# Activations side by side in a SwiGLU channel mixer, a token-major branch merge, and new durations in a list schedule

## The chip, the cores and the metric

The kernel runs on one core of a Trainium2 chip. The metric is the device time of one execution in microseconds (us), as the median of several runs. The profile is one execution taken by the hardware profiler. The engines are PE (TensorE, matrix products), ACT (ScalarE), DVE (VectorE), POOL (GpSimd) and SP (which issues the DMAs); PEld is TensorE's loading of the stationary operand.

## What is computed

One decoder block in float32 for 256 tokens and a model dimension of 1024: three token mixers side by side (sparse attention NSA with 16 heads, an mLSTM, cross-attention to 256 memory tokens), a gated merge, an output projection, and a SwiGLU channel mixer with 2816 hidden features.

```python
h = rmsnorm(x, g_pre_mix)
z = h @ w_in                        # 1024 -> 8248: queries, keys, values, gates of all mixers
...
y_nsa, y_ml, y_mem = ...            # (256, 1024), (256, 512), (256, 512)
gm = sigmoid(g_merge.reshape(B, S, 3, D_MODEL))
y = (gm[:, :, 0] * (y_nsa @ w_proj_nsa) + gm[:, :, 1] * (y_ml @ w_proj_ml)
     + gm[:, :, 2] * (y_mem @ w_proj_mem))
x = x + rmsnorm(y @ w_out, g_post_mix)
h = rmsnorm(x, g_pre_ffn)
gu = h @ w_ffn_in                   # 1024 -> 2 x 2816
gate, up = gu[..., :D_FF], gu[..., D_FF:]
x = x + rmsnorm((silu(gate) * up) @ w_ffn_down, g_post_ffn)
```

## The kernel before

**Numbers in two parts.** Every float32 operand of a large product is split into a high and a low part of the type float32r (`split`: ACT copies the high part, DVE subtracts to get the low one). A product is three matmuls: high by high, high by low, low by high (`mm3`).

**Weights.** They come as 162 units of [128, 1024] in the order of use, one DMA of 512 KB each (`fetch`, tile `raw`, four buffers), and each unit is split into `whi` and `wlo` (four buffers each).

**Two ways to form a product.** With features on the partitions (`fmaj`, `fpair`), a 128x128 block of weights is the stationary operand and the activations of all 256 tokens stream through: 24 matmuls of 256 columns for a tile of 128 features over the 8 tiles of the model dimension. With tokens on the partitions (`tmaj`), a 128x128 block of activations is stationary and 512 columns of weights stream through. `tmaj` works on both halves of the tokens (`tb`), so it holds two PSUM banks at a time and takes each unit of weights first for the one half, then for the other.

**PSUM.** There are eight banks: two with the tag `d`, three `s`, two `t` (transposes), one `v`. `ps_ds` gives out the five of `d` and `s` in turn.

**Stages, in program order.** Memory keys and values; compressed keys and values; gates; memory attention; attention keys and values; then the attention by four groups and two halves of the tokens (`nsa_half`), after each of which `fill` takes some tasks of the list `ORDER`, as many as `FILL` says: mLSTM tasks, then the letters `m`, the merge gates. Before, an `m` is `merge_pair`: two feature tiles of a gate in one bank (12 of them). The merge then goes by eight feature tiles: products of the three branches with their projections, times the sigmoids of the gates, summed and split into `yh` and `yl`. Then come the output projection `w_out` by tokens, the residual `x1` and its transposes, `xh` and `xl`, and the channel mixer: the first 512 gate and up features by tokens (`ffn_gate`, `ffn_up`), the other 18 feature tiles of either kind in pairs by features (`ffn_in`), and the down projection by tokens.

**The order of issue.** The instructions are first recorded in program order. `Plan.schedule` then simulates the engines with a duration for each instruction (`Plan.cost`) and latencies between engines (`LAT`, `SAME`), and on every engine takes the ready instruction that comes first in the program. Buffers of a tag are given out in program order. A tag is made once, with the number of buffers that its first tile names. `issue` then emits all instructions in the order found; no engine can change it at run time.

Of the kernel before, what the change touches and what calls it, by code (L numbers as in the profile page):

```python
# [10 lines left out]
F32 = mybir.dt.float32  # L11
# [6 lines left out]
P = 128  # L18
S = 256          # tokens
D = 1024  # L20
KD = D // P      # feature tiles of the model dimension
# [6 lines left out]
FILL = (5, 7, 1, 2, 3, 1, 3, 2)  # L28
ORDER = "qqvqqsghhhhfmmmmmmmmmmmm"
# [3 lines left out]
# columns of w_in  # L33
C_Q, C_KV, C_G, C_ML, C_IF, C_O, C_QM, C_MG = 0, 1024, 2560, 2608, 4144, 4152, 4664, 5176

# columns of the array of constants
K_ID, K_TRI, K_RV, K_BM, K_M0, K_C1, K_MT, K_END = 0, 128, 256, 257, 261, 533, 549, 677
# columns of the array of gains and small weights
# [4 lines left out]
class View:  # L43
    """A part of a tile that has no place yet."""
# [53 lines left out]

    def region(self):
        """First and last partition, and the elements of a partition as bits."""  # L100
        t = self.tile
        key = repr(self.steps)
        if key not in t.regions:
            p = int(self.ix.flat[0]) // t.n
            bits = np.zeros(t.n, bool)
            bits[self.ix[0].ravel() % t.n] = True
            t.regions[key] = (p, p + self.shape[0], int.from_bytes(np.packbits(bits).tobytes(), "big"))
        return t.regions[key]


class Slot:
    """A tile of the plan: its place is chosen when its first instruction is issued."""
# [50 lines left out]
class Plan:  # L163
    """Records the instructions in program order, with what they read and write, and issues them
    in the order of a list schedule: on every engine the ready one that comes first in the
    program. Tiles of a tag get their buffers in program order."""
# [8 lines left out]
    @contextmanager  # L175
    def later(self, n):
        """The instructions inside come as if n places later in the program."""
        self.boost -= n
        yield
        self.boost += n  # L180
# [47 lines left out]
    def cost(op):  # L228
# [14 lines left out]
        pointers = sum(v.n == 1 for v in op.ins)  # L243
        if op.eng == "ACT":
            return (50 if psum else 95) + 0.833 * n + 93 * ("accum_out" in op.kw or pointers > 0)
        if op.eng == "DVE":
            fast = not psum and op.method in ("tensor_copy", "tensor_scalar")
            return 67 + (0.52 if fast else 1.04) * n + 60 * pointers
# [6 lines left out]
        return 100 + 1.4 * n if op.method == "tensor_scalar" else 150 + 2.1 * n  # L255
# [9 lines left out]
    def schedule(self):  # L265
# [10 lines left out]
        def offer(op):  # L276
            """Makes op a candidate if its new tiles can have places; else it waits for the tag."""
            r = op.ready
            for t in op.tiles:
                if t.real is None:  # L280
                    tag = t.tag
                    if tag.next != t.seq or not tag.free:
                        tag.waiting.setdefault(t.seq, []).append(op)
                        return
                    r = max(r, tag.free[0][0])
            avail[op.eng].append((max(r, held(op)), op))

        def held(op):
            """A bank of PSUM serves one engine at a time, and so do the ports that GpSimd shares."""
# [96 lines left out]
def block_kernel(ctx, tc, order, xN, xT, memT, cst, vec, row, wg, w1, w2, W, out):  # L386
# [75 lines left out]
    def fmaj(out, xs, ks, wu, b0=0, first=True, last=True):  # L462
        """out [128 features, 256] += blocks of a unit (from b0) times the tiles ks of xs."""
# [5 lines left out]

    def fpair(xs, w, i, ps_new=ps_d):  # L470
        """[128, 2, 256]: the i-th pair of feature tiles of the weights w."""
        ps = ps_new([P, 2, S])
        for j in range(2):
            fmaj(ps[:, j, :], xs, range(KD), unit((w, 2 * i + j)))
        return ps

    def tmaj(xs, *key, n=4, ps_new=ps_d, into=None, last=0):
        """[128 tokens, 512] for both halves of the tokens, from n units of two feature tiles each; the
        last ones are used for the first half of the tokens before the second."""
# [29 lines left out]
    def warm_up(n):  # L509
        """Products of no use, that bring the tensor engine's clock up while it would wait."""  # L510
# [4 lines left out]
    def colsum(sq):  # L515
        """[128, 2]: per token, the sum of sq [128, 2, 256] over the partitions and the tiles."""
# [7 lines left out]
    def bcast(r, ps):  # L524
        """ps [128, 256]: the column r [128, 2] of the tokens, on every row."""
# [114 lines left out]
    msk = one.tile([P, 416], BF16, name="msk")          # m0 (272), c1 (16), mt (128)  # L640
# [56 lines left out]
    # running sums of logf, and i - sums  # L697
# [34 lines left out]
    # columns: selected keys 128-255, 0-127, compressed keys, window keys 0-127, 128-255  # L732
    kh = bigt("KK", 2, [P, NG, 528], F32R, "kh")
    kl = bigt("KK", 2, [P, NG, 528], F32R, "kl")
# [61 lines left out]
    for h2 in range(2):  # L796
        pvm = ps_v([P, 2, S], "pvm")
        ptm = [[work.tile([P, 2, S], F32R, tag=f"pT{i}", bufs=2, name="pTm") for i in range(2)] for _ in range(2)]
        for tb in range(2):
# [18 lines left out]
            pt = ps_t([P, 2, 2, P], "ptx")          # m tile, head, t  # L818
# [102 lines left out]
    gm = [bigt("G", 3, [P, 8, S], F32, f"gm{b}") for b in range(3)]  # L921

    def merge_pair(i):
        ps = fpair(X, "g_merge", i)
        ACT.activation(gm[i // 4][:, 2 * (i % 4):2 * (i % 4) + 2, :], ps, AF.Copy)
# [20 lines left out]
    def nsa_half(g, tb, qs, yT):  # L946
# [71 lines left out]
        for e in range(2):  # L1018
# [5 lines left out]
             "h": ml_head, "f": lambda _: ml_finish(), "m": merge_pair}  # L1024
# [16 lines left out]
    last_exp = exps[-12:]  # L1041

    def sigmoids(i):
        for b in range(3):
            g2 = gm[b][:, 2 * i:2 * i + 2, :]
            ACT.activation(g2, g2, AF.Sigmoid, after=last_exp)
# [3 lines left out]
    for fi in range(8):  # L1050
        ps = ps_s([P, 2, S], "pnl")
        pn_, pl_, pm_ = ps[:, 0, :], ps[:, 1, :], ps_t([P, S], "pmm")
        if fi % 2 == 0:
            sigmoids(fi // 2)
        w = unit(("proj", 2 * fi + 1))
        fmaj(pl_, yml, range(4), w)
        fmaj(pm_, ymem, range(4), w, 4)
        fmaj(pn_, (ynh, ynl), range(8), unit(("proj", 2 * fi)))
        m = work.tile([P, 3, S], F32, tag="p", bufs=2, name="mrg")
        for b, x in enumerate((pn_, pl_, pm_)):  # L1060
            DVE.tensor_mul(m[:, b, :], x, gm[b][:, fi, :])
        for b in (1, 2):
            DVE.tensor_add(m[:, 0, :], m[:, 0, :], m[:, b, :])
        split(yh[:, fi, :], yl[:, fi, :], m[:, 0, :])

# [9 lines left out]
    def scaled(name, xs, n, g, z, scale, pre):  # L1075
        """z [128 tokens, 2, 1024]: the products with the units of a name times the gains g and, per token,
        pre; yields per half of the tokens 1/rms of the products times the root of scale."""
# [17 lines left out]
    xh = bigt("KK", 2, [P, KD, S], F32R, "xh")  # L1095
    xl = bigt("KK", 2, [P, KD, S], F32R, "xl")
# [34 lines left out]
    for tb in range(2):  # L1131
# [7 lines left out]
        split(us[0][:, 0, :, t], us[0][:, 1, :, t], pt)  # L1139
    for i in range(4, KF):  # L1140
        ps = fpair((xh, xl), "ffn_in", i, ps_ds)
        sl_ = work.tile([P, S], F32, tag="sq", bufs=3, name="silu")
        DVE.tensor_mul(sl_, ps[:, 0, :], rfb)
        ACT.activation(sl_, sl_, AF.Silu)
        DVE.tensor_mul(sl_, ps[:, 1, :], sl_)
        u = us[i // 4]
        split(u[:, 0, i % 4, :], u[:, 1, i % 4, :], sl_)
# [19 lines left out]
def _layout(inputs):  # L1167
# [10 lines left out]
    def blocks(w, cols, k0=0, k1=None):  # L1178
        """[128, k, cols] of the rows k0..k1 (tiles)."""
# [23 lines left out]
    add_f("g_merge", w_in, tiles(C_MG, 24))  # L1203
    pn, pl, pm = a["w_proj_nsa"][0], a["w_proj_ml"][0], a["w_proj_mem"][0]
    for i in range(8):
        c = slice(i * P, (i + 1) * P)
        units["proj", 2 * i] = blocks(pn, c).reshape(P, 1024)
        units["proj", 2 * i + 1] = np.concatenate([blocks(pl, c), blocks(pm, c)], axis=1).reshape(P, 1024)
    for h in range(2):
        add_t("w_out", a["w_out"][0][:, 512 * h:512 * h + 512], h)  # L1210
# [38 lines left out]
def _stream(units, order):  # L1249
    """The units in the order of their use."""  # L1250
# [27 lines left out]
```

## Time and profile before

| | |
|---|---|
| median of 3 runs | 562.84 us (562.7 to 563.62) |
| profiled execution, span from first to last instruction | 561.4 us |
| mean granted TensorE clock | 0.996 |
| busy: PE, PEld, DVE, ACT, POOL | 551.9, 516.5, 404.5, 334.2, 36.0 us |
| matmuls | 3964 |

The times are of executions without the profiler; of the profiled execution the span is known, which leaves out what lies before its first and after its last instruction. Busy time of PE is the union of matmuls that overlap each other: the profiler gives a matmul of 256 columns some 284 ns from start to end, though the next one starts earlier. All large instructions are recorded by one helper line (L382), so groups are told apart by the names of their tiles: `pd`, `pss`, `pnl` and `pmm` are PSUM banks of large products, `pt...` those of transposes.

### The profile page before, as it was taken

The page shows a single profiled execution, that of the slowest core. Times are in us where ns is not written, and L with a number is a line of the kernel's source. Part 1 is how long each engine was busy: PE and PEld are TensorE (multiplying, and loading weights), DVE is VectorE, ACT ScalarE, POOL GpSimd, SP SyncE. Part 2 cuts the span into 40 slices and gives each one's busy share as a digit, 9 for nine tenths or more (in the row PEclk, how much of TensorE's full clock was granted, in tenths as well). Part 3 has the DMA queues.
Part 4 walks back from the last instruction along what each step waited for, and adds up shares of the span by engine and source line. Part 5 has one row for each costly group of instructions (what it writes and reads, how often), then busy time and mean ns, then how long its engine had stood idle before and what let it go on. Part 6 is the DMA issues. An engine that isn't in the chain of part 4 may idle for free.

```text
span 561.4 us, 10304 instructions
## 1 busy us (share of the span) xinstructions
PE 551.9 (98%) x3964; PEld 516.5 (92%) x3964; DVE 404.5 (72%) x802; ACT 334.2 (60%) x658; POOL 36.0 (6%) x44
## 2 busy tenths in 40 slices
PE   8999999999999999999999999999999999999994
PEld 8899998998989999999999998878999999988883
DVE  4897398598897989987786877865565656654543
ACT  6775677566596858777697444774444444444430
POOL 1110000002002011302111000000000000000000
PEclk9999999999999999999999999999999999999998
DMA  7994327617345253434435655744555545556522
GB/s 246 356 350 154 113 86 228 205 56 238 129 121 180 76 178 124 135 119 160 151 117 158 216 189 188 257 156 123 177 189 183 182 175 179 186 185 191 189 71 75
DMA packets 29281, 95.28 MB, mean 170 GB/s; under 512 B 3376, under 2 KB 6704, under 8 KB 28976
## 3 DMA queue, kind: packets, MB, share of 16 engines
q1 hardware_dynamic: 29232, 94.63, 51.5%
q8 instruction: 31, 0.51, 0.4%
q14 instruction: 18, 0.15, 0.1%
HBM read 92.52 MB, written 1.05 MB: 167 GB/s over the span
## 4 chain that ended last, share of the span: by engine, by line
PE 92%; DMA 3%; ACT 2%; DVE 2%; issue 0%; SPq 0%; DVEq 0%; ACTq 0%
PE pd L382 46%; PE pss L382 23%; PE pnl L382 6%; PE sc L382 3%; PE pvn L382 3%; PE pmm L382 2%; PE ptn L382 2%; DMA memt<-in_memT 2%; PE ph L382 2%; ACT whi L382 1%; DMA raw<-in_W 1%; PE pw L382 1%; PE pn L382 1%; PE pgf L382 1%; PE psm L382 1%; PE pvm L382 1%
## 5 line engine op out<-in xcount | busy, mean ns | idle before, releaser
L382 DVE TENSOR_TENSOR wlo<-raw,whi 128x1024 fp32r<-128x1024 f32 (+1 forms) x161 | 195.4, 1217 | 102.1 <-ACT whi L382 100.7
L382 ACT ACTIVATE whi<-raw 128x1024 fp32r<-128x1024 f32 (+1 forms) x161 | 167.6, 1046 | 164.3 <-issue 72.3
L382 PE MATMUL pd<-hh,whi 128*128 128x256 f32 x416 | 119.7, 288 | 0.3 <-DVE vs L382 0.3
L382 PE MATMUL pd<-hh,wlo 128*128 128x256 f32 x416 | 119.7, 288 | 0.0
L382 PE MATMUL pd<-hl,whi 128*128 128x256 f32 x416 | 119.5, 287 | 0.0
L382 PEld LDWEIGHTS pd<-hh,whi 128*128 128x128 f32 x416 | 79.5, 191 | 0.8 <-DVE vs L382 0.7
L382 PEld LDWEIGHTS pd<-hl,whi 128*128 128x128 f32 x416 | 79.4, 191 | 0.1
L382 PEld LDWEIGHTS pd<-hh,wlo 128*128 128x128 f32 x416 | 79.4, 191 | 0.0
L382 PE MATMUL pss<-xh,wlo 128*128 128x256 f32 x160 | 45.4, 284 | 0.0
L382 PE MATMUL pss<-xl,whi 128*128 128x256 f32 x160 | 45.4, 284 | 0.0
L382 PE MATMUL pss<-xh,whi 128*128 128x256 f32 x160 | 45.4, 283 | 0.0
L382 PE MATMUL pss<-whi,u 128*128 128x512 f32 x132 | 42.4, 392 | 0.0
L382 PE MATMUL pd<-xh,whi 128*128 128x256 f32 x128 | 36.2, 283 | 0.0
L382 PE MATMUL pd<-xl,whi 128*128 128x256 f32 x128 | 36.2, 283 | 0.0
L382 PE MATMUL pd<-xh,wlo 128*128 128x256 f32 x128 | 36.2, 283 | 0.0
L382 PEld LDWEIGHTS pss<-xh,whi 128*128 128x128 f32 x160 | 30.7, 192 | 0.0
L382 PEld LDWEIGHTS pss<-xl,whi 128*128 128x128 f32 x160 | 30.7, 192 | 0.0
L382 PEld LDWEIGHTS pss<-xh,wlo 128*128 128x128 f32 x160 | 30.7, 192 | 0.0
L382 PEld LDWEIGHTS pss<-whi,u 128*128 128x128 f32 x132 | 24.8, 188 | 5.5
L382 ACT ACTIVATE pp<-sc,mx 128x128 f32<-128x128 f32 (+1 forms) x64 | 27.1, 439 | 0.4 <-DVE mx L382 0.3
L382 PE MATMUL pss<-wlo,u 128*128 128x512 f32 x66 | 25.9, 392 | 0.0
L382 DVE TENSOR_REDUCE mx<-sc 128x1 f32<-128x16 f32 (+2 forms) x96 | 22.6, 284 | 3.3 <-PE sc L382 3.0
(306 smaller groups left out, 1243.9 us busy)
## 6 DMA issues: line engine op xcount, KB each, us to landing
raw<-in_W SPq DMA_DIRECT2D x159, 512.0 KB, 3.4
w<-in_w SPq DMA_DIRECT2D x2, 1024.0 KB, 7.0
raw<-in_W SPq DMA_DIRECT2D x6, 256.0 KB, 5.6
xt<-in_xT SPq DMA_DIRECT2D x2, 512.0 KB, 7.6
x<-in_xN SPq DMA_DIRECT2D x2, 512.0 KB, 4.9
out<-z SPq DMA_DIRECT2D x8, 128.0 KB, 2.0
memt<-in_memT SPq DMA_DIRECT2D x6, 128.0 KB, 5.4
wgt<-in_wg SPq DMA_DIRECT2D x1, 512.0 KB, 6.3
```

Of the source, the lines that this page charges most:

```text
L382: op.ins_ = getattr(op.real, op.method)(*map(arg, op.a), **{k: arg(x) for k, x in op.kw.items()})
```

## The change

**Channel mixer.** `xh` and `xl` become the two halves of one tile `xc` [128, 8, 2, 256] (and the attention's `kh` and `kl`, which hold its place before, two halves of `kk_`). For the 36 feature tiles of `ffn_in`, a new `fcat` multiplies each block of high weights with `xc[:, k]`, 512 columns at once, and the low weights with the high activations alone, 256 columns. The bank then holds two partial sums; `joined` copies the second with ACT and adds the first with DVE. Each feature tile has a bank of its own, where a gate and an up tile shared one.

**Merge by tokens.** The merge gates and the three projections are formed with `tmaj`, in halves of 512 features. `merge_half` replaces `merge_pair` (six instead of twelve), the merged result is by tokens and is transposed back, sixteen 128x128 transposes into banks `pty`, before the split. `ORDER` has 6 letters `m`, and `FILL` places one after each of the last six attention halves. The weights are laid out to match; their number of units stays 162.

**Durations.** `Plan.cost` gets other figures for ACT, DVE and POOL, and a new term for instructions on a part of the partitions.

```diff
-FILL = (5, 7, 1, 2, 3, 1, 3, 2)
-ORDER = "qqvqqsghhhhfmmmmmmmmmmmm"
+FILL = (5, 7, 1, 1, 1, 1, 1, 1)
+ORDER = "qqvqqsghhhhfmmmmmm"
...
+    def place(self):
+        return int(self.ix.flat[0]) // self.tile.n % P, self.shape[0]
...
+        part = any(v.place() != (0, P) and v.shape[0] >= 32 for v in op.outs + [v for v in op.ins if v.n > 1])
         if op.eng == "ACT":
-            return (50 if psum else 95) + 0.833 * n + 93 * ("accum_out" in op.kw or pointers > 0)
+            return ((50 if psum else 95) + 10 + 0.833 * n + 93 * ("accum_out" in op.kw) + 93 * (pointers > 0)
+                    + 110 * part)
         if op.eng == "DVE":
             fast = not psum and op.method in ("tensor_copy", "tensor_scalar")
-            return 67 + (0.52 if fast else 1.04) * n + 60 * pointers
+            return 71 + (0.52 if fast else 1.04) * n + 60 * (0 if n == 1 else pointers) + 100 * part
...
-        return 100 + 1.4 * n if op.method == "tensor_scalar" else 150 + 2.1 * n
+        return 100 + 1.4 * n if op.method == "tensor_scalar" else 2.1 * n - 70
...
+    def fcat(xc, w, ps):
+        hi, lo = unit(w)
+        b = lambda k: slice(k * P, (k + 1) * P)
+        for k in range(KD - 1):
+            PE.matmul(ps, hi[:, b(k)], xc[:, k], start=k == 0, stop=False)
+        for k in range(KD):
+            PE.matmul(ps[:, 0, :], lo[:, b(k)], xc[:, k, 0], start=False, stop=False)
+        PE.matmul(ps, hi[:, b(KD - 1)], xc[:, KD - 1], start=False, stop=True)
+        return ps
...
-    kh = bigt("KK", 2, [P, NG, 528], F32R, "kh")
-    kl = bigt("KK", 2, [P, NG, 528], F32R, "kl")
+    kk_ = bigt("KK", 1, [P, 2, NG, 528], F32R, "kk")
+    kh, kl = kk_[:, 0], kk_[:, 1]
...
-    gm = [bigt("G", 3, [P, 8, S], F32, f"gm{b}") for b in range(3)]
-    def merge_pair(i):
-        ps = fpair(X, "g_merge", i)
-        ACT.activation(gm[i // 4][:, 2 * (i % 4):2 * (i % 4) + 2, :], ps, AF.Copy)
+    gm = [bigt("G", 3, [P, 2, D], F32, f"gm{b}") for b in range(3)]
+    def merge_half(i):
+        b, h = i % 3, i // 3
+        for tb, ps in enumerate(tmaj(X, "g_merge", b, h)):
+            ACT.activation(gm[b][:, tb, 512 * h:512 * h + 512], ps, AF.Copy)
...
-    def sigmoids(i):
-        for b in range(3):
-            g2 = gm[b][:, 2 * i:2 * i + 2, :]
-            ACT.activation(g2, g2, AF.Sigmoid, after=last_exp)
-    for fi in range(8):
-        ps = ps_s([P, 2, S], "pnl")
-        pn_, pl_, pm_ = ps[:, 0, :], ps[:, 1, :], ps_t([P, S], "pmm")
-        if fi % 2 == 0:
-            sigmoids(fi // 2)
-        w = unit(("proj", 2 * fi + 1))
-        fmaj(pl_, yml, range(4), w)
-        fmaj(pm_, ymem, range(4), w, 4)
-        fmaj(pn_, (ynh, ynl), range(8), unit(("proj", 2 * fi)))
-        m = work.tile([P, 3, S], F32, tag="p", bufs=2, name="mrg")
-        for b, x in enumerate((pn_, pl_, pm_)):
-            DVE.tensor_mul(m[:, b, :], x, gm[b][:, fi, :])
-        for b in (1, 2):
-            DVE.tensor_add(m[:, 0, :], m[:, 0, :], m[:, b, :])
-        split(yh[:, fi, :], yl[:, fi, :], m[:, 0, :])
+    for h in range(2):
+        c = slice(512 * h, 512 * h + 512)
+        m = [work.tile([P, 1024], F32, tag="p", bufs=2, name="mrg") for _ in range(2)]
+        for b, name, xs, n in ((1, "proj_ml", yml, 2), (2, "proj_mem", ymem, 2), (0, "proj_nsa", (ynh, ynl), 4)):
+            g2 = gm[b][:, :, c]
+            ACT.activation(g2, g2, AF.Sigmoid, after=last_exp)
+            for tb, ps in enumerate(tmaj(xs, name, h, n=n, ps_new=ps_ds)):
+                acc, new = m[tb][:, 0:512], m[tb][:, 512:1024]
+                if b == 1:
+                    DVE.tensor_mul(acc, ps, gm[b][:, tb, c])
+                else:
+                    DVE.tensor_mul(new, ps, gm[b][:, tb, c])
+                    DVE.tensor_add(acc, acc, new)
+        for tb in range(2):
+            pt = ps_t([P, 4, P], "pty")
+            for j in range(4):
+                PE.transpose(pt[:, j, :], m[tb][:, j * P:(j + 1) * P], ident)
+            t = slice(tb * P, (tb + 1) * P)
+            split(yh[:, 4 * h:4 * h + 4, t], yl[:, 4 * h:4 * h + 4, t], pt)
...
-    xh = bigt("KK", 2, [P, KD, S], F32R, "xh")
-    xl = bigt("KK", 2, [P, KD, S], F32R, "xl")
+    xc = bigt("KK", 1, [P, KD, 2, S], F32R, "xc")
+    xh, xl = xc[:, :, 0], xc[:, :, 1]
...
+    def joined(ps):
+        t = work.tile([P, S], F32, tag="sq", bufs=6, name="join")
+        ACT.activation(t, ps[:, 1, :], AF.Copy)
+        DVE.tensor_add(t, t, ps[:, 0, :])
+        return t
     for i in range(4, KF):
-        ps = fpair((xh, xl), "ffn_in", i, ps_ds)
-        sl_ = work.tile([P, S], F32, tag="sq", bufs=3, name="silu")
-        DVE.tensor_mul(sl_, ps[:, 0, :], rfb)
-        ACT.activation(sl_, sl_, AF.Silu)
-        DVE.tensor_mul(sl_, ps[:, 1, :], sl_)
+        gate = joined(fcat(xc, ("ffn_in", 2 * i), ps_ds([P, 2, S])))
+        DVE.tensor_mul(gate, gate, rfb)
+        ACT.activation(gate, gate, AF.Silu)
+        up = joined(fcat(xc, ("ffn_in", 2 * i + 1), ps_ds([P, 2, S])))
+        DVE.tensor_mul(up, gate, up)
         u = us[i // 4]
-        split(u[:, 0, i % 4, :], u[:, 1, i % 4, :], sl_)
+        split(u[:, 0, i % 4, :], u[:, 1, i % 4, :], up)
...
-    add_f("g_merge", w_in, tiles(C_MG, 24))
-    pn, pl, pm = a["w_proj_nsa"][0], a["w_proj_ml"][0], a["w_proj_mem"][0]
-    ...
+    for b in range(3):
+        for h in range(2):
+            c = C_MG + 1024 * b + 512 * h
+            add_t("g_merge", w_in[:, c:c + 512], b, h)
     for h in range(2):
+        for b in ("nsa", "ml", "mem"):
+            add_t("proj_" + b, a["w_proj_" + b][0][:, 512 * h:512 * h + 512], h)
```

More of the change, by code (lines that the diff above doesn't have):

```diff
@@ L1023, in block_kernel @@
     tasks = {"q": ml_qk, "s": lambda _: ml_silu(), "g": lambda _: ml_gate(), "v": lambda _: ml_values(),
-             "h": ml_head, "f": lambda _: ml_finish(), "m": merge_pair}
+             "h": ml_head, "f": lambda _: ml_finish(), "m": merge_half}
     todo = [lambda t=t, i=ORDER[:i].count(t): tasks[t](i) for i, t in enumerate(ORDER)]
@@ L1202, in _layout @@
     add_f("q_nsa", w_in, tiles(C_Q, 8))
-    add_f("g_merge", w_in, tiles(C_MG, 24))
-    pn, pl, pm = a["w_proj_nsa"][0], a["w_proj_ml"][0], a["w_proj_mem"][0]
[L1205 to L1208, printed above, removed]
+    for b in range(3):
+        for h in range(2):
+            c = C_MG + 1024 * b + 512 * h
+            add_t("g_merge", w_in[:, c:c + 512], b, h)
     for h in range(2):
+        for b in ("nsa", "ml", "mem"):
+            add_t("proj_" + b, a["w_proj_" + b][0][:, 512 * h:512 * h + 512], h)
         add_t("w_out", a["w_out"][0][:, 512 * h:512 * h + 512], h)
```

## The prediction

> **What bounds the kernel now.** I read the page first: span, busy shares and slices.
>
> ```profile
> span 561.4 us, 10304 instructions
> PE 551.9 (98%) x3964; PEld 516.5 (92%) x3964; DVE 404.5 (72%) x802; ACT 334.2 (60%) x658; POOL 36.0 (6%) x44
> PE   8999999999999999999999999999999999999994
> PEclk9999999999999999999999999999999999999998
> PE 92%; DMA 3%; ACT 2%; DVE 2%; issue 0%; SPq 0%; DVEq 0%; ACTq 0%
> ```
>
> TensorE is busy in every slice, at the full granted clock, and it is 92% of the chain that ended last. DVE at 72% has room. So the time is the number of matmuls times the spacing of their starts, plus the few places where TensorE waits. The busy time can't give the spacing, since matmuls overlap. I took it from the timeline of TensorE, with two windows beside it.
>
> ```profile
> 400.00:440.00 40.00, 40.00 (x336) 40.00 (x335) 24.50 (x36) 18.86 (x28) 0.00 (x0) 1.00 0.55 181
> 126.00:134.00 8.00, 8.00 (x37) 6.62 (x36) 7.66 (x17) 3.57 (x4) 4.17 (x2) 1.00 0.67 209
> ```
>
> ```profile
> 395.57 0.28 PE L382 MATMUL pd<-xh,whi 128*128 128x256 f32 x1
> ...
> 399.89 0.28 PE L382 MATMUL pd<-xh,whi 128*128 128x256 f32 x1
> ```
>
> ```profile
> 386.00 0.39 PE L382 MATMUL pss<-wlo,xh 128*128 128x512 f32 x1
> ...
> 388.27 0.39 PE L382 MATMUL pss<-whi,xl 128*128 128x512 f32 x1
> ```
>
> A row of the timeline gives start and duration; only starts are used. The columns of the windows are PE, PEld, DVE, ACT and POOL busy, clock, DMA share and GB/s. In the channel mixer (400 to 440) TensorE runs 336 matmuls of 256 columns in 40 us, and the weight loads fill all 40 us. In the token-major value products (126 to 134) the loads fill 6.62 of 8 us. From 395.57 to 399.89 lie 36 starts: 120.0 ns for a matmul of 256 columns. From 386.00 to 388.27 lie 10 starts: 227 ns for one of 512. Two of 256 cost 240 ns, one of 512 does the same columns in 227: **13 ns are saved for each pair that becomes one**. This is the whole lever of the change, and it is small: 5.4% of the converted work.
>
> By the Trainium skill (TensorE: Matmul & The Clock Gate, Back-to-back issue gap), warm starts lie N/2.4 + 2.5 ns apart, which would be 109.2 and 215.8 ns, 2.5 ns saved for a pair; by that estimate the 768 pairs below would save 1.9 us in all. The trace differs (120.0 and 227 ns), and the rows are used here.
>
> **The change part by part.**
>
> *Channel mixer.* The 36 feature tiles of `ffn_in` (18 pairs) each take 24 matmuls of 256 columns now, 8 k tiles by 3. After, `fcat` multiplies the high weights once with xh and xl side by side (8 of 512 columns) and the low weights with xh (8 of 256). The tile goes from 24 x 0.120 = 2.88 us to 8 x 0.227 + 8 x 0.120 = 2.776 us. Times 36: **-3.7 us**.
>
> *Merge gates.* 24 feature tiles of 24 matmuls (576 of 256) become 6 halves of 2 x 8 x 3 (288 of 512): 69.1 to 65.4 us, **-3.7 us**.
>
> *Branch projections.* 8 tiles of 48 matmuls (384 of 256) become 2 x 16 x 2 x 3 = 192 of 512: 46.1 to 43.6 us, **-2.5 us**.
>
> The merged result is then by tokens, and 16 transposes bring it back, in four groups of four. The nearest rows are the four `ptu` transposes among matmuls of 256:
>
> ```profile
> 389.41 0.28 PE L382 MATMUL pss<-xl,whi 128*128 128x256 f32 x1
> 389.54 0.60 PE L382 MATMUL ptu<-cs,ut 128*128 128x128 f32 x4
> 389.89 0.36 PE L382 MATMUL pss<-xh,wlo 128*128 128x256 f32 x1
> 390.09 0.28 PE L382 MATMUL pss<-xh,whi 128*128 128x256 f32 x1
> ```
>
> From 389.41 to 390.09 pass 0.68 us for two matmuls (0.24) and the group: 0.44 us with the slow start of the next matmul. Four groups: **+1.8 us**. Matmuls and transposes together: -3.7 - 3.7 - 2.5 + 1.8 = **-8.1 us**.
>
> The 512 spacing is not the same everywhere. In the down projection it is:
>
> ```profile
> 500.22 0.62 PE L382 MATMUL pss<-whi,u 128*128 128x512 f32 x2
> ...
> 502.31 0.63 PE L382 MATMUL pss<-whi,u 128*128 128x512 f32 x2
> ```
>
> Nine starts in 2.09 us, 232 ns. If all 768 new matmuls ran so, 768 x 5 ns = 3.8 us would go again. I take 227, since the mixer's neighbour in time (386 to 388) has it; the other end stays for the range.
>
> *DVE and ACT in the mixer.* Rows of the groups by shape (count, busy us, mean ns, idle before):
>
> ```profile
> L382 DVE TENSOR_TENSOR wlo<-raw,whi 128x1024 fp32r<-128x1024 f32 x155 | 191.2, 1238 | 100.4 <-ACT whi L382 99.0 <-PE ptn L382 0.7
> L382 ACT ACTIVATE whi<-raw 128x1024 fp32r<-128x1024 f32 x155 | 163.8, 1062 | 163.5 <-issue 72.3 <-PE pd L382 47.8 <-PE pss L382 24.5
> L382 DVE TENSOR_TENSOR silu<-pss,rfb 128x256 f32<-128x256 f32 x10 | 4.2, 424 | 3.4 <-PE pss L382 3.4
> L382 ACT ACTIVATE pTm<-ptx 128x256 fp32r<-128x256 f32 x8 | 2.6, 383 | 0.0
> ```
>
> `joined` adds to each tile one ACT copy of 128x256 from PSUM (383 ns) and one DVE add (424). By the window 400 to 440, 40/2.88 = 13.9 tiles took 24.5 us of DVE, 1.76 each, and 1.36 of ACT. After: 2.19 of 2.78 us on DVE (79%) and 1.74 on ACT (63%). Both stay under TensorE, so I cost them at nothing. Without that cover the adds would be 36 x 0.42 = 15 us. Each tile now takes a PSUM bank of its own, in a ring of five: its reader has four tiles, 11 us, before TensorE needs it again. The three `sq` places (the `bufs=6` comes after the tag was made with 3, so three it stays) suffice: the third tile after one comes 8.3 us later, and copy, add, multiply and split are four or five instructions of about 0.4 us with one 1.24 us weight split or two between. `xc` takes the places of kh and kl in one piece; their last readers are the attention's scores, long done. On SP nothing changes but the content: 162 units of weights before and after, each one transfer.
>
> *DVE and ACT in the merge.*
>
> ```profile
> L382 DVE TENSOR_TENSOR mrg<-mrg 128x256 f32<-128x256 f32 x16 | 6.7, 421 | 0.2
> L382 DVE TENSOR_TENSOR pTl<-ptn,pTh 128x512 fp32r<-128x512 f32 x24 | 15.6, 682 | 3.3 <-ACT pTh L382 3.1
> L382 ACT ACTIVATE pTh<-ptn 128x512 fp32r<-128x512 f32 x24 | 13.3, 597 | 4.6 <-PE ptn L382 4.6
> ```
>
> DVE goes from 48 instructions of 0.42 us to 24 of 0.68, 20.2 to 16.4 us, and ACT's sigmoids from 12 to 6 of twice the width. TensorE hides both, so this is worth nothing. But the end of the merge is longer. Before, the last products ended so:
>
> ```profile
> 342.55 0.76 DVE L382 TENSOR_TENSOR mrg<-pnl,gm 128x256 f32<-128x256 f32 x2 [0.28 <-PE pnl L382]
> 345.34 1.06 ACT L382 ACTIVATE whi<-raw 128x1024 fp32r<-128x1024 f32 x1 [1.80 <-PE pss L382]
> 347.58 0.42 DVE L382 TENSOR_TENSOR yl<-mrg,yh 128x256 fp32r<-128x256 f32 x1
> ```
>
> 5.45 us from multiply to split, hidden by three of `w_out`'s four units. After, multiply, add, four transposes and two splits are 0.68 + 0.68 + 0.44 + 0.60 + 0.68 = 3.1 us, with the same weight splits between and the way to TensorE and back: some 6 to 8 us. Only units 0 and 1 of `w_out`, whose rows come from the first half, don't need it: 24 x 0.227 = 5.4 us, and 1.4 us more for each token half's own turn. TensorE may wait 0 to 1 us; I take 0.4.
>
> *Bank turnover of the gates.* A gate pair used one `d` bank at a time; a half holds both, and they end 6 matmuls (1.4 us) apart. The next user of `d` waits for an ACT copy. The profile shows such an end, of the NSA values:
>
> ```profile
> 100.91 0.39 PE L382 MATMUL pd<-whi,hl 128*128 128x512 f32 x1
> 101.33 0.60 ACT L382 ACTIVATE vs<-pd 128x512 fp32r<-128x512 f32 x1 [0.76 <-PE pd L382]
> 101.59 0.39 PE L382 MATMUL pd<-hh,whi 128*128 128x256 f32 x1 [0.29 <-DVE vs L382]
> ```
>
> 0.68 us between starts where 0.227 is due: 0.45 lost, where nothing else was ready. Six halves: 0 to 2.7 us. Between them the attention's scores and transposes stand ready to fill, so I take 0.17 each, **+1.0 us**. Behind the copies on ACT are the weight splits, four units ahead.
>
> *Durations in the planner.* They change no instruction, only the order of issue and which buffers are taken when. No row shows a price; TensorE's only wait in these rows is a single 0.45 us, so I bound it at -1 to +1.5 us and take 0. Fewer, longer gate tasks (`FILL`, six of 48 x 0.227 = 10.9 us, one after each half) move the filler of the attention's halves; before it was 1, 2, 3, 1, 3, 2 pairs of 48 x 0.120 = 5.8 us. I cost this at nothing: the filler as a whole shrinks by 5% only.
>
> **The sum.** -8.1 + 0.4 + 1.0 = -6.7 us: a span of 554.7 us. The profiled execution's own time isn't shown; its span lies 1.4 us under the median of the three runs (562.84), which I carry over: **556.1 us**.
>
> **The rivals.**
>
> *Half the gain goes to waits.* Spacing of 232 ns in the new matmuls (+3.8), 1 us at the merge's end and 2.7 at the banks: -8.1 + 3.8 + 1 + 2.7 = -0.6 at the extreme; with half of the first, -2.5: 560.3 us. For it: the 232 ns row and the 0.45 us row; against it: 227 ns on both sides of the mixer's start.
>
> *The columns alone bind.* If the starts followed the columns and a matmul of 256 took half of one of 512, the pairs would save nothing; the transposes (+1.8) and the waits (+1.4) would be left: 566.0 us. The rows speak against it: 120.0 ns held over 36 starts with nothing between, and twice that is not 227. By the page's rule named above, which is nearly this case, the pairs' 1.9 us and the 1.8 us of the transposes would cancel.
>
> *Slower: the gates' banks starve TensorE.* At each half's end the copy on ACT can stand behind weight splits, as two in a row here:
>
> ```profile
> 303.98 2.25 ACT L382 ACTIVATE whi<-raw 128x1024 fp32r<-128x1024 f32 x2 [1.93 <-PE pnl L382]
> ```
>
> From the last matmul's start to a free bank would pass 0.42 (100.91 to 101.33 above) + 2.25 + 0.60 = 3.3 us; less the 1.4 us in which the other bank is still being filled, 1.9 us a half. Six halves make 11.4 us instead of my 1.0: 566.5 us. It decides from 6.7/6 + 0.17 = 1.3 us a half. Against it: gate pairs in a row stopped TensorE nowhere, and in the attention other matmuls stand ready.
>
> **How the numbers follow.** The forecast has 0.73; its own range is 553.7 us (no waits, order -1) to 558.6 us (spacing 229 ns, +1.5; waits of 2.4 instead of 1.4). Waits and spacing that eat half have 0.15, the columns alone 0.03, the starving 0.04; 0.05 is left for the order of issue eating most of the gain. A change of 0.2%, 1.1 us, is about what the measurement can tell from none. Faster by more than that: 0.73 + 0.13 + 0.01 = 0.87; within it 0.02 + 0.04 = 0.06; slower 0.07. For 8 in 10 I take 553.2 to 560.2 us: nearly all of the forecast's chance and two thirds of the first rival's.
>
> **What would show it.** The profile after should have some 3212 matmuls (3964 - 768 + 16); rows of 512 columns with xc, 288, starting 227 ns apart; the mixer's tiles 2.78 us apart; DVE there near 79%; four groups of transposes into `pty`; PEld's share well under 92%. The forecast is wrong if TensorE's starts show gaps over 0.3 us at the ends of gate halves, at `w_out`'s third unit, or if 512 columns with weights as the stationary side take over 232 ns.

## The result, and the profile after

The changed kernel takes 557.20 us in the median of 4 runs (556.56 to 558.98) against 563.16 us before (562.70 to 563.62): a ratio of 0.9897, with a 95% interval of 0.9879 to 0.9916. The forecast was 556.1 us, faster. The profiled execution took 557.31 us; its span is 5.9 us shorter than before.

The page of the changed kernel: span, busy shares, slices of TensorE and its clock, shares of the chain that ended last.

```profile
span 555.5 us, 8864 instructions
PE 544.0 (98%) x3212; PEld 476.3 (86%) x3212; DVE 416.3 (75%) x814; ACT 347.3 (63%) x684; POOL 30.6 (6%) x44
PE   8999999999999999999999999999999999999994
PEclk9999999999999999999999999999999999999998
PE 89%; DVE 4%; DMA 2%; ACT 2%; issue 1%; SPq 1%; DVEq 0%; ACTq 0%
```

TensorE still bounds the kernel, at the same clock, with the 3212 matmuls foreseen. Its share of the last chain fell from 92% to 89%, and DVE's rose from 2% to 4%: a little more of the time goes to waiting (2.3 us of idle time before, 4.2 after, by the lists of waits). The window of 400 to 440 us, in the mixer (columns as in the prediction):

```profile
400.00:440.00 40.00, 40.00 (x233) 35.32 (x233) 32.26 (x50) 24.72 (x43) 0.00 (x0) 1.00 0.52 192
```

233 matmuls where there were 336, the weight loads down from 40.00 to 35.32 us, DVE up from 24.50 to 32.26 us (81% of the window) and TensorE busy throughout. Two tiles there, in TensorE's timeline, where a row gives the start, the time to the last end, and how many matmuls it joins:

```profile
441.71 1.11 PE L388 MATMUL pd<-xc,wlo 128*128 128x256 f32 x8
442.66 2.00 PE L388 MATMUL pd<-xc,whi 128*128 128x512 f32 x8
444.50 1.12 PE L388 MATMUL pd<-xc,wlo 128*128 128x256 f32 x8
445.46 0.40 PE L388 MATMUL pd<-xc,whi 128*128 128x512 f32 x1
```

Eight starts of 256 columns take 0.95 us (119 ns each), eight of 512 take 1.84 us (230 ns), one tile 2.79 us. Where TensorE waits now (releaser: us in all, times, longest):

```profile
PE warm L388 <- POOL ones L388: 1.0, 1, 1.0
PE pd L388 <- DVE vml L388: 1.0, 1, 1.0
PE pss L388 <- ACT whi L388: 0.5, 1, 0.5
PE pss L388 <- DVE xc L388: 0.4, 1, 0.4
...
PE pss L388 <- ACT xc L388: 0.2, 1, 0.2
```

The second row is new (the rows left out are of 0.2 to 0.3 us each), and belongs to a place that the change doesn't touch in the program, the mLSTM values:

```profile
132.04 3.19 DVE L388 TENSOR_TENSOR wlo<-raw,whi 128x1024 fp32r<-128x1024 f32 x2
...
134.55 0.39 PE L388 MATMUL pd<-whi,hl 128*128 128x512 f32 x1
...
135.16 0.68 DVE L388 TENSOR_TENSOR vml<-pd,vml 128x512 fp32r<-128x512 f32 x1
...
135.89 0.39 PE L388 MATMUL pd<-hh,whi 128*128 128x256 f32 x1 [0.95 <-DVE vml L388]
```

DVE does two weight splits ahead of the split of `vml`, which has to empty the bank. 1.34 us pass between starts where 0.23 is due. The same place before, where the split of `vml` came first. TensorE's last product of the values started at 134.55 there too, so it lost 0.19 us; scores came next, which need no bank `d`:

```profile
134.25 0.69 DVE L382 TENSOR_TENSOR vml<-pd,vml 128x512 fp32r<-128x512 f32 x1 [0.58 <-ACT vml L382]
134.86 1.22 DVE L382 TENSOR_TENSOR wlo<-raw,whi 128x1024 fp32r<-128x1024 f32 x1
...
134.97 0.39 PE L382 MATMUL sc<-kh,qs 128*128 128x256 f32 x1
```

The other large new place is between the output projection and the first hidden features, where TensorE waits for ACT and DVE to make `xc`, 0.22 and 0.43 us, against one wait of 0.16 us before (before, then after):

```profile
365.33 0.74 PE L382 MATMUL pd<-wq,xh 128*128 128x512 f32 x2 [0.16 <-ACT xh L382]
```

```profile
362.09 0.73 PE L388 MATMUL pss<-wq,xc 128*128 128x512 f32 x2 [0.22 <-ACT xc L388]
...
363.25 3.03 PE L388 MATMUL pss<-wq,xc 128*128 128x512 f32 x12 [0.43 <-DVE xc L388]
```

From the starts of the first output projection and of the first down projection, before and after in turn,

```profile
342.35 0.40 PE L382 MATMUL pd<-whi,yh 128*128 128x512 f32 x1
...
388.86 0.36 PE L382 MATMUL pss<-xh,whi 128*128 128x256 f32 x1
...
493.49 0.39 PE L382 MATMUL pss<-whi,u 128*128 128x512 f32 x1
```

```profile
338.16 0.39 PE L388 MATMUL pss<-whi,yh 128*128 128x512 f32 x1
...
386.06 0.94 PE L388 MATMUL pd<-xc,whi 128*128 128x512 f32 x3
...
487.59 0.39 PE L388 MATMUL pss<-whi,u 128*128 128x512 f32 x1
```

and the first product of the mixer's pairs (388.86 before, 386.06 after), the 5.9 us divide so:

| stretch | before | after | difference |
|---|---|---|---|
| start to the output projection | 342.35 | 338.16 | -4.19 |
| output projection to the mixer | 46.51 | 47.90 | +1.39 |
| mixer (18 pairs) | 104.63 | 101.53 | -3.10 |
| down projection to the end | 67.94 | 67.94 | 0.00 |

### The profile page after: what moved, and what is told of

It is laid out like the page before. It is cut to its first block, busy times and chain, and to the rows that moved or that the text cites. A ratio compares the mean times of both kernels' runs of the same rounds, so it can differ in the third digit from the quotient of the medians.

```text
span 555.5 us, 8864 instructions
## 1 busy us (share of the span) xinstructions
PE 544.0 (98%) x3212; PEld 476.3 (86%) x3212; DVE 416.3 (75%) x814; ACT 347.3 (63%) x684; POOL 30.6 (6%) x44
## 4 chain that ended last, share of the span: by engine, by line
PE 89%; DVE 4%; DMA 2%; ACT 2%; issue 1%; SPq 1%; DVEq 0%; ACTq 0%
PE pd L388 46%; PE pss L388 30%; PE sc L388 3%; PE pvn L388 3%; PE ptn L388 2%; PE ph L388 2%; DMA mraw<-in_cst 1%; DVE wlo L388 1%; DVE cy L388 1%; DMA raw<-in_W 1%; ACT whi L388 1%; PE pw L388 1%; PE pgf L388 1%; PE psm L388 1%; PE pvm L388 1%
## 5 line engine op out<-in xcount | busy, mean ns | idle before, releaser
L388 PE MATMUL pd<-hh,whi 128*128 128x256 f32 x224 | 64.7, 289 | 1.2 <-DVE vml L388 1.0
L388 PE MATMUL pd<-hh,wlo 128*128 128x256 f32 x224 | 64.0, 286 | 0.0
L388 PE MATMUL pd<-hl,whi 128*128 128x256 f32 x224 | 63.7, 284 | 0.0
L388 PE MATMUL pd<-wlo,hh 128*128 128x512 f32 x144 | 57.9, 402 | 0.0
L388 PE MATMUL pd<-whi,hl 128*128 128x512 f32 x144 | 57.6, 402 | 0.0
L388 PE MATMUL pd<-whi,hh 128*128 128x512 f32 x144 | 57.6, 403 | 0.0
L388 PEld LDWEIGHTS pd<-hh,whi 128*128 128x128 f32 x224 | 42.9, 191 | 2.2 <-DVE vml L388 1.4
L388 PE MATMUL pss<-xc,whi 128*128 128x512 f32 x168 | 43.2, 392 | 0.0
L388 PEld LDWEIGHTS pd<-hl,whi 128*128 128x128 f32 x224 | 42.9, 191 | 0.1
L388 PEld LDWEIGHTS pd<-hh,wlo 128*128 128x128 f32 x224 | 42.8, 191 | 0.0
```

Source lines behind the costliest of these rows:

```text
L388: op.ins_ = getattr(op.real, op.method)(*map(arg, op.a), **{k: arg(x) for k, x in op.kw.items()})
```

## The experiments

Ratios are to the kernel before, with 95% intervals; "mixer" is the third stretch of the table.

**The parts alone.** First the mixer by itself: `xc`, `fcat`, `joined` and the loop over `ffn_in` of the diff, with the old merge and durations.

> The kernel before with the channel mixer's change alone (high and low activations side by side, joined afterwards). If the gain is the spacing of starts (theory): 288 pairs of matmuls become one each; at 10 to 13 ns a pair the mixer is 2.9 to 3.7 us shorter and so is the run, about 559.9 us. If the order of issue by the new durations brought the gain (rival): no change here, 563.1 us.

559.78 us (559.38 to 561.01), ratio 0.9950 [0.9938, 0.9962]. The mixer takes 101.53 us, as in the whole change, and the span ends 3.4 us earlier. The theory held: this part carries its own gain and disturbs nothing.

The merge by itself, on the kernel before with its durations:

```diff
-FILL = (5, 7, 1, 2, 3, 1, 3, 2)
-ORDER = "qqvqqsghhhhfmmmmmmmmmmmm"
+FILL = (5, 7, 1, 1, 1, 1, 1, 1)
+ORDER = "qqvqqsghhhhfmmmmmm"
...             (and merge_half, the halves of the projections, pty)
```

> The kernel before with the merge by tokens alone (gates, projections, transposes, FILL and ORDER). Theory: 480 pairs at 10 to 13 ns save 4.8 to 6.2 us, sixteen transposes cost 1.8, waits 0 to 1: 2.0 to 4.4 us faster, about 560 us. Rival, that the gate halves' banks make TensorE wait: 0.3 us or more of gap at the end of each half, 562 us or slower.

562.48 us (561.28 to 563.42), ratio 0.9991 [0.9983, 1.0000]: almost nothing, against 2.0 to 4.4 us expected. The output projection does start 4.2 us earlier, at 338.17. The gain is lost behind it, between the output projection and the mixer (TensorE's timeline):

```profile
363.38 0.73 PE L386 MATMUL pss<-wq,xh 128*128 128x512 f32 x2 [1.50 <-ACT xh L386]
364.53 0.50 PE L386 MATMUL pss<-wq,xl 128*128 128x512 f32 x1 [0.42 <-DVE xl L386]
...
371.86 0.50 PE L386 MATMUL pss<-wq,xh 128*128 128x512 f32 x1 [0.78 <-ACT xh L386]
```

These waits, 2.7 us of idle time, are some 3.2 us of late starts; with the eight transposes of the second feature half (0.87 us) they eat the 4.2 us. Neither the theory nor its rival, banks of the gates, had this place. No wait stands at the ends of gate halves.

The durations by themselves, on the kernel before:

> The kernel before with the new durations in the planner alone. Theory: no instruction changes; the wait of about 1 us that the changed kernel shows after the mLSTM values comes from the order on DVE, so it stands here too and the run is 0 to 1 us slower, about 563.7 us. Rival, that the durations carry part of the gain: 561 us or less.

562.24 us (561.67 to 562.99), ratio 0.9986 [0.9978, 0.9995]. The wait for `vml` is here too, 0.96 us at 136.20 us, so it comes from the new durations, not from the merge or the mixer. But the run is not slower, as the theory had it, nor as fast as the rival's 561 us: it is 0.7 us faster in the medians, 0.3 us in the profiled spans. The theory overlooked what the new order gains nearby. Added up in the trace from each matmul's start to the next one's, the products of the normalized input and the attention between them take 237.65 us before and 237.02 here, the 0.9 us lost at `vml` included: the new order gains some 1.5 us there and gives 0.9 back. And the changed kernel with the three old formulas of `Plan.cost`:

> The changed kernel with the old durations back in the planner. Theory: the wait after the mLSTM values is gone, 0 to 1 us faster than the changed kernel, about 556.5 us. Rival, that the durations carry part of the gain: 558 us or more. If the three parts add up, the gains of the mixer alone and the merge alone sum to this one's.

558.70 us (558.14 to 559.95), ratio 0.9930 [0.9917, 0.9944]. The wait for `vml` is gone, but the waits behind the output projection are back:

```profile
PE pss L386 <- ACT xc L386: 1.5, 2, 0.8
```

The expectation, faster than the whole change, missed, and the rival (558 us or more) held: with the merge the new durations are worth 1.5 us. The parts don't add. Alone they shorten the span by 3.4, 0.3 and 0.3 us, together by 5.9: most of the merge's gain appears only with the new order of issue.

**What a pair of 256 is worth.** Each matmul of 512 columns in `fcat` goes as two of 256 again, everything else as changed:

```diff
-            PE.matmul(ps, hi[:, b(k)], xc[:, k], ...)
+            for j in range(2):
+                PE.matmul(ps[:, j, :], hi[:, b(k)], xc[:, k, j], ...)
```

> The changed kernel with each matmul of 512 columns in the mixer done as two of 256 (high weights by xh into the one half of the bank, by xl into the other); layout, banks and joining stay. Theory: the mixer's tile goes back from 2.77 to 2.88 us, so 36 tiles give back 3.2 to 3.9 us: about 560.7 us, all of it between the last transposes of the first 512 hidden features and the first down product. Rival, that layout and banks, not the spacing, brought the gain: 557.2 us.

560.37 us (560.05 to 561.39), ratio 0.9955 [0.9938, 0.9971]. The mixer takes 104.63 us, that of the kernel before: all of its gain is in the pairs, 3.10 us / 288 = 10.8 ns each. The weight loads fill the window again:

```profile
400.00:440.00 40.00, 40.00 (x336) 40.00 (x335) 31.15 (x49) 24.17 (x42) 0.00 (x0) 1.00 0.53 182
```

**What the transposes cost.** Each is done twice: `for j in (0, 1, 2, 3, 0, 1, 2, 3)`.

> The changed kernel with the merge's sixteen transposes issued twice. Theory: 16 x 0.109 = 1.7 us slower, about 558.9 us, within the merge and the output projection. Rival, that transposes run in gaps of TensorE: 557.2 us.

559.53 us (559.10 to 559.56), ratio 0.9935 [0.9920, 0.9950]. The output projection starts 0.87 us later, and the stretch of the second feature half is another 0.87 us longer: 0.109 us for a transpose, 1.74 for the sixteen, where the prediction had 1.8. About 0.45 us more went to longer waits for `xc` at 364 to 365 us (0.48 and 0.62). They can't be put down to the transposes: the kernel with pairs of 256, whose transposes are single, has waits of 0.50 and 0.62 us there.

**How much cover DVE has in the mixer.** `joined` gets one more instruction of DVE, and in another kernel two, that copy `ps[:, 0, :]` to a tile nobody reads:

```diff
+            DVE.tensor_copy(spare, ps[:, 0, :])
```

> The changed kernel with one more DVE instruction of 128x256 from PSUM for each of the mixer's 36 tiles (a copy that nobody reads). Theory: DVE goes from about 79% to 94% of the mixer and stays under TensorE: no change, 557.2 us. Rival, that DVE is already on the path there: up to 36 x 0.42 = 15 us slower.

> As the one before, with two more copies a tile. Theory: DVE needs 2.19 + 2 x 0.42 = 3.03 us a tile where TensorE needs 2.77, so DVE becomes the bound: 36 x 0.26 = 9 us slower, about 566 us, and TensorE's matmuls show gaps. Rival, that there is more slack than the busy time shows: no change.

558.10 us (557.48 to 560.02), ratio 0.9917 [0.9893, 0.9941], and 558.88 us (557.78 to 560.60), ratio 0.9925 [0.9897, 0.9954]. The mixer takes 101.52 us in both, unchanged; their spans grew at other places, the first weights at 16 to 17 us and the waits for `xc` behind the output projection; why these vary is not shown. With one copy the theory held for the time; DVE's share was 86%, not 94%. With two, it had DVE as the bound, and this failed. Windows of the changed kernel, of the one with one copy and of the one with two, and the latter's largest group of copies (columns as in the prediction):

```profile
400.00:480.00 80.00, 80.00 (x461) 70.44 (x461) 64.25 (x101) 49.75 (x87) 0.00 (x0) 1.00 0.52 188
```

```profile
400.00:480.00 80.00, 80.00 (x460) 70.41 (x459) 68.53 (x130) 50.63 (x87) 0.00 (x0) 1.00 0.56 189
```

```profile
400.00:480.00 80.00, 80.00 (x459) 70.32 (x458) 75.49 (x157) 49.06 (x86) 0.00 (x0) 1.00 0.53 180
L388 DVE COPY spare<-pss 128x256 f32<-128x256 f32 x42 | 17.5, 417 | 0.0
```

With two copies, 56 more instructions on DVE, each 417 ns from start to end, add 11.2 us of busy time, 201 ns apiece. Two things make it so little: an instruction behind a copy starts 0.33 us after it, before it has ended, and the copies fill pauses of DVE between instructions that need each other's result (in the changed kernel 35 to 70 ns each). So a sum of durations overstates DVE's load. At 94% busy it still delays nobody.

**Order within a tile.** Matmuls of 512 and 256 columns in turn instead of seven, eight and one:

```diff
-        for k in range(KD - 1):
-            PE.matmul(ps, hi[:, b(k)], xc[:, k], ...)
         for k in range(KD):
+            if k < KD - 1:
+                PE.matmul(ps, hi[:, b(k)], xc[:, k], ...)
             PE.matmul(ps[:, 0, :], lo[:, b(k)], xc[:, k, 0], ...)
```

> The changed kernel with the mixer's matmuls of 512 and 256 columns in turn (high of k, low of k, ...) instead of seven of 512, eight of 256, one of 512. In the changed kernel the first 256 after a 512 starts 113 ns before its successor and the others 120, and the six matmuls of 512 after the run of 256 take 228 to 236 ns and the next ones 227. Theory, that loads of weights that were held up in the run of 256 are paid by the 512s after it: in turn no run builds up, each pair takes 113 + 227 = 340 ns instead of some 350, 36 x 8 x 7 to 10 ns = 2 to 3 us faster. Rival, that each kind keeps its mean (231 and 119): no change, 557.2 us.

557.95 us (557.73 to 560.86), ratio 0.9924 [0.9899, 0.9948]. The theory failed: the mixer is 0.93 us longer (102.46) and not 2 to 3 us shorter.

```profile
440.16 0.40 PE L388 MATMUL pd<-xc,whi 128*128 128x512 f32 x1
440.40 0.28 PE L388 MATMUL pd<-xc,wlo 128*128 128x256 f32 x1
...
441.92 0.40 PE L388 MATMUL pd<-xc,whi 128*128 128x512 f32 x1
```

Five couples in 1.76 us, 352 ns each, where 512 and 256 in runs take 230 + 119 = 349. Runs of one shape are the better order here, by a little.

**The waits that are left.** Two edits to the changed kernel. The NSA and mLSTM values use their last two units of weights for the first token half before the second, so that the first bank is emptied while the second is still being filled. And the residual with its transposes and the making of `xc` is placed 200 instructions earlier in the program order of the planner:

```diff
-    for tb, ps in enumerate(tmaj(X, "v_nsa")):
+    for tb, ps in enumerate(tmaj(X, "v_nsa", last=2)):
...
-        for tb, ps in enumerate(tmaj(X, "v_ml")):
+        for tb, ps in enumerate(tmaj(X, "v_ml", last=2)):
...
+        with plan.later(-200):
             for q in range(2):
                 DVE.scalar_tensor_tensor(x1[:, tb, c], z[:, tb, c], r, x1[:, tb, c], ...)
```

> The changed kernel with two edits against its own waits. One: the NSA and mLSTM values take their last two units of weights for the first half of the tokens before the second, so that the first bank has 2.7 us instead of 1.4 to be emptied. Theory: the gaps at 101 us (0.45 us) and 134.6 us (1.1 us) go: 1.5 us. Two: the residual, its transposes and the splits after the output projection come 200 places earlier in the planner's program, so that the first half's transposes don't stand behind all matmuls of the second half. Theory: the gaps from 361 to 364 us go, 1.0 to 1.3 us. Together about 554.6 us. Rival, that the gaps come back at the next user of the same banks or splits: 556.5 us or more.

**554.43 us (553.80 to 554.73), ratio 0.9843 [0.9826, 0.9860]**, faster than both kernels. The span is 552.0 us. All of TensorE's waits, and the place of the former waits for `xc`:

```profile
PE warm L388 <- POOL ones L388: 1.0, 1, 1.0
PE pd L388 <- DVE wlo L388: 0.2, 1, 0.2
PE pss L388 <- ACT whi L388: 0.2, 1, 0.2
```

```profile
356.21 0.60 PE L388 MATMUL ptx<-cs,x 128*128 128x128 f32 x4
...
359.39 5.41 PE L388 MATMUL pss<-wq,xc 128*128 128x512 f32 x23
```

The transposes of `x1` now stand among the last matmuls of the output projection, and the hidden features follow without a wait. The output projection starts at 335.80, 2.4 us earlier than in the changed kernel, and the mixer, 101.52 us long as in the changed kernel, 3.5 us earlier. Of the 2.4 us, 0.65 lie ahead of the first edit, in waits for the first weights and a smaller one at 45 us (the last product of the NSA values starts at 100.44 instead of 101.09), so they are not the edits'. At the two values 0.45 and 1.1 us of late starts are gone, behind the output projection 1.2 us, about as expected. The waits at the values and behind the output projection were thus worth 2.8 us (557.20 to 554.43); the two edits were not run one by one.

To see whether the residual's place alone explains the loss in the merge by itself, the second edit was made to that kernel, with the old durations:

> The kernel before with the merge by tokens alone, old durations, and the residual after the output projection 200 places earlier in the planner's program. The merge alone reached the output projection 4.2 us earlier and lost 3.2 us of it again in gaps between that projection and the first hidden features (361 to 372 us). Theory, that those gaps come from the place of the residual, its transposes and splits in the order, which the new durations happen to mend: they go here without the new durations, 3 us faster than the merge alone, about 559.4 us. Rival, that the merge's banks or the later split of its second half cause them: 562 us or more.

561.45 us (561.35 to 561.76), ratio 0.9964 [0.9951, 0.9978]: 1.0 us came back of the 3 that the theory gave, so it failed for the most part; the rival, 562 us or more, missed too. The first wait fell from 1.50 to 0.45 us; the third stayed:

```profile
361.75 0.74 PE L386 MATMUL pss<-wq,xh 128*128 128x512 f32 x2 [0.45 <-ACT xh L386]
362.91 0.50 PE L386 MATMUL pss<-wq,xl 128*128 128x512 f32 x1 [0.42 <-DVE xl L386]
...
370.25 0.73 PE L386 MATMUL pss<-wq,xh 128*128 128x512 f32 x2 [0.78 <-ACT xh L386]
```

DVE shows why, in this kernel and then in the changed one:

```profile
365.07 2.36 DVE L386 TENSOR_TENSOR wlo<-raw,whi 128x1024 fp32r<-128x1024 f32 x2 [0.33 <-ACT whi L386]
367.35 1.41 DVE L386 SCALAR_TENSOR_TENSOR x<-z,ss,x 128x512 f32<-128x512 f32 x2
```

```profile
364.93 1.40 DVE L388 SCALAR_TENSOR_TENSOR x<-z,ss,x 128x512 f32<-128x512 f32 x2
366.25 2.35 DVE L388 TENSOR_TENSOR wlo<-raw,whi 128x1024 fp32r<-128x1024 f32 x2
```

With the old durations the residual of the second token half comes behind two weight splits, with the new ones ahead of them. The changed kernel with the old durations has the old order as well (residual at 367.85, behind two weight splits), and its third wait is 0.78 us too. That is the order which the new durations buy in the presence of the merge.

**Where the 512-column spacing comes from.** In the changed kernel the projections of the memory branch run at 232 to 233 ns, those of the mLSTM and NSA branches at 227 to 228. The two pools of SBUF are made in the other order, so that the large tiles and the weight buffers change places. The 3212 matmuls and transposes come in the same order in both traces:

```diff
+    wpool = pool("wpool", 1)
     big = pool("big", 1)
-    wpool = pool("wpool", 1)
```

> The changed kernel with two SBUF pools in the other order: the buffers of weights lie low (31 to 80 KB) and the large activations above them. In the changed kernel the down projection's matmuls of 512 take 232 ns with the hidden tiles u0 to u2 as stationary side, which lie at 31 to 64 KB, and 227 ns with u3 to u5, which lie above 72 KB; so with the memory branch's result (40 KB, 232 ns) and the mLSTM's (64 KB, 227 ns). Theory, that the place of the stationary tile sets it: all of these at 227 ns, 144 x 5 ns = 0.7 us less in the down projection. Rival, that the place in the stream of instructions sets it: the same pattern as before.

559.09 us (558.78 to 559.72), ratio 0.9927 [0.9909, 0.9945]. The two stretches changed their spacing; after, and with the pools swapped:

```profile
299.76 0.40 PE L388 MATMUL pss<-wlo,ymemt 128*128 128x512 f32 x1
...
301.16 0.39 PE L388 MATMUL pss<-wlo,ymemt 128*128 128x512 f32 x1
```

```profile
299.98 0.39 PE L388 MATMUL pss<-wlo,ymemt 128*128 128x512 f32 x1
...
301.34 0.39 PE L388 MATMUL pss<-wlo,ymemt 128*128 128x512 f32 x1
```

Six starts in 1.40 and in 1.36 us, 233 and 227 ns. By medians of the starts, the memory projections went from 232 to 227 ns, and those of the mLSTM and NSA branches and the output projection the other way, from 227 to 232. Two other runs on the same chip with the pools in the first order keep 232 and 227, so the chip is not the reason. So the place of the operands decides between the two spacings; neither the theory nor the rival foresaw an exchange. The rule that the theory gave (above 64 KB of a partition it is 227 ns) does not fit: the swap moves all large tiles up by the weight buffers, twelve of 4 KB a partition. The mLSTM's, which the expectation places at 64 KB, comes to 112 KB and is slow there. The 0.7 us hoped for in the down projection were 0.1 (67.82 us). What the rule is stays open.

## Why the prediction was right

It was right in its mechanism and nearly in its sum (-6.7 us of span forecast, -5.9 measured), but two of its waits stood at the wrong place, and several errors cancelled by luck, as the items show.

- **Pairs of 256 to 512: right.** The mixer gained 3.1 us of the 3.7 forecast. The size was off because 512 columns take 230 ns there and not 227; the pair is worth 10.8 ns, not 13. The spacing at 386 to 388 us, which the prediction chose, did not hold 50 us later; the 232 ns row that it kept for the other end was nearer. In the tile at 442.66 the eight starts lie 234, 235, 229, 232, 231, 227, 226 and 227 ns apart: what is over 227 stands in the five behind the run of 256. Why they are slower is not shown. The Trainium skill (TensorE: Matmul & The Clock Gate, Back-to-back issue gap) gives N/2.4 + 2.5 ns for the isolated gap, 2.5 ns saved a pair, which by an estimate is 0.7 us for the mixer's 288, and about 131 ns for 512 columns in a stream with weight loads. The trace agrees with neither: 10.8 ns a pair, 3.1 us, and 230 ns.
- **Gates and projections: right in sum, in part by luck.** Up to the output projection the forecast was -3.7 - 2.5 + 0.9 (half of the transposes) + 1.0 (banks) = -4.3, and -4.19 was measured. The terms are less exact. Added up from start to start, the projections went from 45.88 us (384 matmuls, 119.5 ns each) to 44.05 (192, 229 ns each): 1.8 us and not 2.5, in part since the memory branch runs at 232 ns. The gates bear the same names as other products of the normalized input; these and the attention between them took 237.65 us before and 234.50 in the merge alone, 3.15 us less where the gates and their banks were to give 2.7. The new durations took another 0.8 us out of this stretch and lost 0.9 at `vml`. That all this came within 0.1 us of the forecast is luck.
- **Bank turnover of the gates, +1.0: wrong, nothing.** No wait stands at the end of a gate half, in the changed kernel or the merge alone. In the timeline the attention's matmuls stand between those of the gates, so the ends are filled; the row that the prediction took, of the NSA values, is a place where nothing else was ready.
- **End of the merge, +0.4 at `w_out`'s third unit: wrong place, and the size by luck.** TensorE does not wait there. The wait is 20 us later, at the making of `xc`: 0.22 + 0.43 - 0.16 = 0.5 us more. The prediction followed the merge's chain to the first stage behind it and stopped; it did not ask what an earlier output projection leaves late next, the residual with its norm, transposes and splits on ACT and DVE.
- **Transposes, +1.8: right.** 1.74 by the kernel that does them twice.
- **Durations, 0: the term that failed as a sum.** 0.3 us of span gained alone, 1.5 us gained with the merge, and a new 1.1 us gap inside that. The bounds of -1 to +1.5 were too narrow on the side of a gain, and the step took for granted that parts can be costed one by one. The order of issue is worth what the other edits make late.
- **DVE and ACT hidden in the mixer: right.** DVE is at 81% where 79% was forecast, and at 94%, with two more copies a tile, it was hidden too.
- **Rivals.** That half the gain goes to waits is partly what the merge alone does, at another place than the banks. The columns alone are excluded by the kernel that splits the pairs again, and the starving by the list of waits.

## What to carry to other kernels

Where TensorE is busy throughout, take the spacing from the starts of its rows, in the stage that the change touches and in its steady part, and count gains per converted pair: here 10.8 ns times their number in the mixer, 9.5 in the projections, no more. Then follow an earlier stage past its first consumer to the next handover, and move what is late there (here the residual, 200 places earlier, and the first bank's emptying) before the next matmul is optimised: those two edits gave 2.8 us, about as much as the 288 pairs. And an edit to a scheduler's costs must be timed together with the edits that it is meant for.

## What the runs showed of the hardware

- Matmuls of 512 columns with a fresh stationary operand start 227 or 232 ns apart in this kernel, depending on where their operands lie in SBUF. Swapping two pools inverted it (medians: 232 to 227 for the memory projections, 227 to 232 for the mLSTM's and NSA's and for the output projection). Nothing was gained by the swap: the mixer was 0.6 us longer, at 102.11.
- DVE instructions of 417 ns, put between others that need each other's result, added 201 ns each to its busy time.
- Weight loads are busy for 100% of a window of 256-column matmuls (40.00 of 40 us) and for 88% where two thirds of the columns go by 512 (35.32 of 40 us).
